# Gate and up products by seven block products instead of eight, with the activations in token halves

## The chip, the cores and the metric

One core of one Trainium2 chip runs the kernel. The metric is the device time in microseconds (us); the kernel before has a median of 1925.08 us over three runs (1923.73 to 1928.44).

## The reference, cut to what matters

A decoder trunk of two layers on 512 tokens with 1024 channels, float32. Each layer is a half-step FFN, an attention, and a half-step FFN, so there are four FFNs, which carry most of the arithmetic:

```python
x = x + 0.5 * swiglu(rms_norm(x, gain), w_gate_up, w_down)      # four times
h = rms_norm(x, gain)                                            # ahead of each attention
x = x + stick_breaking_attention(h, ...)   # layer 0
x = x + sliding_window_attention(h, ...)   # layer 1

def swiglu(h, w_gate_up, w_down):          # 1024 -> 2 x 2816 -> 1024
    gate, up = jnp.split(h @ w_gate_up, 2, axis=-1)
    return (jax.nn.silu(gate) * up) @ w_down
```

## The kernel before, in words

Activations stand transposed: 8 tiles of 128 channels x 512 tokens. Every float32 operand is split exactly into a high and a low part, and a product of two operands is three passes on TensorE (PE): high x high, high x low, low x high. The weights are the stationary operand, the tokens stream past them, 512 a matmul.

Weights come as a stream of units of 128 x 1024 (512 KB). SyncE (SP) issues the load of a unit into a `raw` tile, ScalarE (ACT) copies it to the high part `whi` (L181), VectorE (DVE) subtracts for the low part `wlo` (L186; in the attentions two halves on GpSimd (POOL), L184). There are three buffers of each; `release`, called after the last matmul of a unit, starts the work on the unit three further on. So ACT and DVE prepare one unit while PE works on another.

An FFN (`ffn`) runs over 22 columns f of 128 hidden channels. For each there is a gate and an up product, each 8 channel tiles x 3 passes = 24 matmuls of 128 x 512 into one PSUM bank (`gu`). `swiglu` then multiplies both by the row factor of the norm `rbc` (L307, L309), takes silu on ACT, multiplies (L310) and splits the result into `hh` and `hl` (L313, L314). After all columns come 8 output tiles `dn` of 22 x 3 matmuls, each added to x (L300). `norm_tile` splits each new x tile into `xh` (L252, ACT) and `xl` (L253, DVE) and adds up its squares (L260 on ACT, L261 on POOL for the first six tiles). The row factor is made late: `norm_rows` sums squares on PE (`ss`) and takes the reciprocal root in eleven small DVE operations (`nv`, `nr`, `nt`); `norm_bcast` spreads it over the partitions (`dgh`, `dgl`, `bc`, `rbc`). One 24-matmul product stands between `ss` and `bc` to cover that.

The order on PE is the program's order. On the other engines a scheduler orders the instructions by when their inputs come.

Of the kernel before, what the change touches and what calls it, by code (L numbers as in the profile page):

```python
# [22 lines left out]
DOWN = (8, 7, 7)  # L23
# [5 lines left out]
UNITS = 3  # L29
WARM = 40  # L30
# [9 lines left out]
# 500000 ** (-arange(0, 16, 2) / 16) in float32  # L40
# [24 lines left out]
class _Ordered:  # L65
    """an engine whose instructions stay in the order of the program"""
# [40 lines left out]

class _Trunk:
    def __init__(self, tc, pools, psum, aps):
        self.tc, self.nc = tc, _Engines(tc)  # L110
        self.const, self.work = pools
        self.psum = psum
        self.aps = aps
        self.units = []
        self.raw, self.ready = [], []
        self.taken = self.spent = 0
        self.roped = False
        self.extra = -1

# [28 lines left out]
    def queue(self, ap, pool=False):  # L148
        self.units.append((ap, ap.shape[1], pool))

    def _load(self, pieces=1):
        n = len(self.raw)
        if n < len(self.units):
            ap = self.units[n][0]
            raw = self.work.tile([P, ap.shape[1]], F32, tag="raw", name=f"raw{n}", bufs=UNITS)
            self.raw.append(raw)
            if pieces == 1:
                self.nc.sync.dma_start(raw, ap)

    def _open(self, n):  # L160
        size = self.units[n][1]
        hi = self.work.tile([P, size], F32R, tag="whi", name=f"whi{n}", bufs=UNITS)
        lo = self.work.tile([P, size], F32R, tag="wlo", name=f"wlo{n}", bufs=UNITS)
        self.ready.append((hi, lo))

    def advance(self, hi, lo):
        """one more unit of the weight stream ahead, in tiles that the stage has free"""
        n = self.extra = len(self.ready)
        self.ready.append((hi, lo))
        self._part(n)  # L170
        self._load()

    def _part(self, n, i=0, pieces=1):
        nc, (ap, size, pool) = self.nc, self.units[n]
        size //= pieces
        s = slice(i * size, (i + 1) * size)
        hi, lo = self.ready[n]
        raw = self.raw[n]
        if pieces > 1:
            nc.sync.dma_start(raw[:, s], ap[:, s])  # L180
        nc.scalar.copy(hi[:, s], raw[:, s])  # L181
        if pool and pieces == 1:
            for t in (slice(0, size // 2), slice(size // 2, size)):
                nc.gpsimd.tensor_sub(lo[:, t], raw[:, t], hi[:, t])  # L184
        else:
            nc.vector.tensor_sub(lo[:, s], raw[:, s], hi[:, s])  # L186

    def release(self, count):
        self.spent += count
        ahead = UNITS + (self.spent <= self.extra)  # L190
        while count and len(self.ready) < min(self.spent + ahead, len(self.units)):
            n = len(self.ready)
            self._open(n)
            self._part(n)
            self._load()

    def weights(self, a):
# [3 lines left out]
        h3, l3 = (t.rearrange("p (a b) -> p a b", a=a) for t in (hi, lo))  # L201
        return [(h3[:, i, :], l3[:, i, :]) for i in range(a)]

# [1 line left out]
    def setup(self, which):  # L205
# [4 lines left out]
        bank = self.psum.tile([P, T], F32, tag="tr", name="warmup", bufs=2)  # L210
# [5 lines left out]
        for n in range(UNITS):  # L216
            self._load(2)
            self._open(n)
        for half in range(2):
            for m in range(4):  # L220
                k = 4 * half + m
                nc.sync.dma_start(self.x[k], aps["xt"][k])
                if m < UNITS:
                    self._part(m, half, 2)
                self.norm_tile(k, which)
        for _ in range(UNITS):
            self._load()
# [16 lines left out]
    def norm_tile(self, k, which):  # L244
        nc, w = self.nc, self.work
        if k == 0:
            self.xh, self.xl = [], []
            self.acc = w.tile([P, T], F32, tag="acc", name="acc", bufs=1)
        g = self.gain[:, which * KD + k : which * KD + k + 1]
        hi = w.tile([P, T], F32R, tag=f"xh{k}", name=f"xh{k}", bufs=1)  # L250
        lo = w.tile([P, T], F32R, tag=f"xl{k}", name=f"xl{k}", bufs=1)
# [3 lines left out]
        self.xl.append(lo)  # L255
        if k == 0:
            nc.scalar.activation(self.acc, self.x[k], AF.Square)
        else:
            sq = w.tile([P, T], F32, tag="rbc", name="sq", bufs=1)
            nc.scalar.activation(sq, self.x[k], AF.Square)  # L260
            (nc.gpsimd if k < POOL_SQUARES else nc.vector).tensor_add(self.acc, self.acc, sq)  # L261

# [10 lines left out]
    def norm_rows(self):  # L273
# [4 lines left out]
        v = w.tile([P, TB], F32, tag="nv", name="nv", bufs=1)  # L278
        r = w.tile([P, TB], F32, tag="nr", name="nr", bufs=1)
        tmp = w.tile([P, TB], F32, tag="nt", name="nt", bufs=1)  # L280
# [4 lines left out]
    def norm_bcast(self):  # L285
        nc, w = self.nc, self.work
        bc = self.psum.tile([P, T], F32, tag="tr", name="bc", bufs=2)
# [8 lines left out]
        self.rbc = w.tile([P, T], F32, tag="rbc", name="rbc", bufs=1)  # L296
# [6 lines left out]
    def swiglu(self, fp, f, gu):  # L303
        nc = self.nc
        g = fp.tile([P, T], F32, tag="g", name="g", bufs=2)
        u = fp.tile([P, T], F32, tag="u", name="u", bufs=2)
        nc.vector.tensor_mul(g, gu[0], self.rbc)  # L307
        nc.scalar.activation(g, g, AF.Silu)
        nc.vector.tensor_mul(u, gu[1], self.rbc)  # L309
        nc.vector.tensor_mul(u, g, u)  # L310
        hi = fp.tile([P, T], F32R, name=f"hh{f}")
        lo = fp.tile([P, T], F32R, name=f"hl{f}")
        nc.scalar.copy(hi, u)  # L313
        nc.vector.tensor_sub(lo, u, hi)  # L314
        return hi, lo

    def ffn(self, following, first=False, rope=False):
        tc, nc = self.tc, self.nc
        with tc.tile_pool(name="ffn", bufs=1) as fp:
            hs, evac = [], []  # L320
            xs = list(zip(self.xh, self.xl))
            ahead = []
            if first:
                ahead = [(self.bank("gu"), self.weights(KD)) for _ in range(3)]
                for half in range(2):
                    ks = range(half * KD // 2, (half + 1) * KD // 2)
                    for k, (m, (ps, w)) in [(k, t) for k in ks for t in enumerate(ahead)] if half == 0 else [
                        (k, t) for t in enumerate(ahead) for k in ks
                    ]:
                        self.mm3(ps, [(w[k], xs[k])], first=(k == 0), last=(k == KD - 1), release=1 if k == KD - 1 else ())  # L330
                        if k == KD - 1 and m == 1:
                            self.norm_rows()
                ahead = [ps for ps, _ in ahead]
            for f in range(NF):
                gu = []
                for s in range(2):
                    u = 2 * f + s
                    if ahead:
# [691 lines left out]
```

## Time and profile before

| what | value |
|---|---|
| median of three runs | 1925.08 us |
| span of the profiled execution | 1925.5 us |
| PE busy / DVE / ACT / POOL, share of the span | 98% / 50% / 36% / 9% |
| mean granted TensorE clock | 0.992 |
| one FFN's gate/up products behind the first column | 228.5 us |
| one FFN's down products | 123.2 us |

The profiled execution's span and the median of the runs differ by 0.4 us, so sums against the span can be set beside the median as they are. A matmul's duration in the profile is longer than its spacing, since matmuls overlap; times per matmul are taken from the length of a run of them, not from the mean duration.

### The profile page before, as it was taken

How to read it: one execution, taken by the hardware profiler on the slowest of the kernel's cores; microseconds unless marked ns; L12 is line 12 of the kernel's file. 1: busy time of each engine (PE TensorE's matmuls, PEld its weight loads, DVE VectorE, ACT ScalarE, POOL GpSimd, SP SyncE). 2: the span in 40 equal slices, each digit the busy share in tenths (PEclk: the TensorE clock that was granted, in tenths of full speed). 3: DMA queues.
4: the chain of work that ended last, by engine and by line, in shares of the span. 5: the costliest groups of instructions: out<-in, count | busy, mean ns of one | idle time of the engine just before them, and what ended most of it. 6: DMA issues, size and time to landing. Idle time of an engine off the chain costs nothing.

```text
span 1925.5 us, 22581 instructions
## 1 busy us (share of the span) xinstructions
PE 1895.7 (98%) x8994; PEld 1565.6 (81%) x8994; DVE 970.5 (50%) x1535; ACT 695.1 (36%) x1071; POOL 172.0 (9%) x131
## 2 busy tenths in 40 slices
PE   9999999999999999999999999999998999999999
PEld 7888888877887888888888888888887788888887
DVE  6444433378887644443235444423588664444321
ACT  5333222266675323332223333222357542223211
POOL 1000000233321000000000000000142210000000
PEclk9999999999999999999999999999989999999999
DMA  5233333321112333223333222333221122332331
GB/s 167 98 97 99 96 91 92 103 69 56 49 62 66 99 97 97 92 97 94 97 96 99 92 98 96 93 93 100 81 67 34 29 92 98 99 99 90 103 109 60
DMA packets 49930, 170.52 MB, mean 89 GB/s; under 512 B 5921, under 2 KB 6177, under 8 KB 49825
## 3 DMA queue, kind: packets, MB, share of 16 engines
q1 hardware_dynamic: 49824, 169.07, 27.9%
q8 instruction: 71, 1.16, 0.2%
q14 instruction: 35, 0.28, 0.0%
HBM read 166.96 MB, written 2.10 MB: 88 GB/s over the span
## 4 chain that ended last, share of the span: by engine, by line
PE 84%; DVE 8%; issue 4%; ACT 3%; POOL 1%; DMA 0%; SPq 0%; ACTq 0%; DVEq 0%; POOLq 0%
PE gu L75 49%; PE dn L75 23%; PE op L75 4%; PE tok L75 3%; DVE keep L459 2%; DVE beta L460 1%; PE pv L75 1%; DVE qs L376 1%; DVE wt L482 1%; ACT keep L453 1%; PE sc L75 1%; PE z L75 0%; PE ptr L75 0%; DVE e L793 0%; PE q L75 0%
## 5 line engine op out<-in xcount | busy, mean ns | idle before, releaser
L181 ACT CAST whi<-raw 128x1024 fp32r<-128x1024 f32 (+2 forms) x323 | 330.0, 1022 | 964.8 <-issue 361.6
L75 PE MATMUL gu<-xh,whi 128*128 128x512 f32 x1400 | 545.5, 390 | 1.4 <-ACT whi L181 1.4
L75 PE MATMUL gu<-xh,wlo 128*128 128x512 f32 x1400 | 545.0, 389 | 0.7 <-DVE wlo L186 0.7
L75 PE MATMUL gu<-xl,whi 128*128 128x512 f32 x1400 | 544.8, 389 | 0.5 <-DVE xl L253 0.5
L186 DVE TENSOR_TENSOR wlo<-raw,whi 128x1024 fp32r<-128x1024 f32 (+2 forms) x293 | 349.4, 1193 | 248.2 <-ACT whi L181 245.6
L75 PEld LDWEIGHTS gu<-xh,wlo 128*128 128x128 f32 x1400 | 262.8, 188 | 56.5 <-DVE wlo L186 1.8
L75 PEld LDWEIGHTS gu<-xh,whi 128*128 128x128 f32 x1400 | 262.9, 188 | 56.2 <-ACT whi L181 1.9
L75 PEld LDWEIGHTS gu<-xl,whi 128*128 128x128 f32 x1400 | 262.9, 188 | 55.3 <-DVE xl L253 0.9
L75 PE MATMUL dn<-hh,wlo 128*128 128x512 f32 x704 | 280.9, 399 | 0.0
L75 PE MATMUL dn<-hl,whi 128*128 128x512 f32 x704 | 277.4, 394 | 0.0
L75 PE MATMUL dn<-hh,whi 128*128 128x512 f32 x704 | 276.0, 392 | 0.0
L309 DVE TENSOR_TENSOR u<-gu,rbc 128x512 f32<-128x512 f32 x87 | 60.1, 691 | 274.7 <-PE gu L75 274.7
L75 PEld LDWEIGHTS dn<-hl,whi 128*128 128x128 f32 x704 | 132.1, 188 | 34.3
L75 PEld LDWEIGHTS dn<-hh,whi 128*128 128x128 f32 x704 | 132.2, 188 | 31.5
L75 PEld LDWEIGHTS dn<-hh,wlo 128*128 128x128 f32 x704 | 132.2, 188 | 30.5
L307 DVE TENSOR_TENSOR g<-gu,rbc 128x512 f32<-128x512 f32 x88 | 60.8, 691 | 176.5 <-PE gu L75 176.4
L261 POOL TENSOR_TENSOR acc<-acc,sq 128x512 f32<-128x512 f32 x30 | 46.4, 1547 | 1116.1 <-ACT sq L260 1116.1
L184 POOL TENSOR_TENSOR wlo<-raw,whi 128x512 fp32r<-128x512 f32 x60 | 87.5, 1483 | 164.9 <-ACT whi L181 164.9
L75 PE MATMUL tok<-whi,xh 128*128 128x256 f32 x288 | 86.4, 300 | 0.0
L75 PE MATMUL tok<-whi,xl 128*128 128x256 f32 x288 | 82.4, 286 | 0.1
L75 PE MATMUL tok<-wlo,xh 128*128 128x256 f32 x288 | 82.3, 286 | 0.1
L300 DVE SCALAR_TENSOR_TENSOR x<-dn,x 128x512 f32<-128x512 f32 x32 | 22.1, 691 | 116.5 <-PE dn L75 116.5
(310 smaller groups left out, 1957.4 us busy)
## 6 DMA issues: line engine op xcount, KB each, us to landing
raw<-in_gu_dram SPq DMA_DIRECT2D x173, 512.0 KB, 3.4
raw<-in_dn_dram SPq DMA_DIRECT2D x64, 448.0 KB, 3.3
raw<-in_dn_dram SPq DMA_DIRECT2D x32, 512.0 KB, 3.5
raw<-in_sbqk_dram SPq DMA_DIRECT2D x16, 512.0 KB, 3.4
raw<-in_swin_dram SPq DMA_DIRECT2D x10, 512.0 KB, 3.5
raw<-in_sbv_dram SPq DMA_DIRECT2D x8, 512.0 KB, 3.3
raw<-in_sbo_dram SPq DMA_DIRECT2D x8, 512.0 KB, 3.5
raw<-in_swo_dram SPq DMA_DIRECT2D x8, 512.0 KB, 3.3
```

What stands on the lines that cost most here:

```text
L75: return self._tc.keep_in_program_order(method(*args, **kwargs))
L181: nc.scalar.copy(hi[:, s], raw[:, s])
L184: nc.gpsimd.tensor_sub(lo[:, t], raw[:, t], hi[:, t])
L186: nc.vector.tensor_sub(lo[:, s], raw[:, s], hi[:, s])
L261: (nc.gpsimd if k < POOL_SQUARES else nc.vector).tensor_add(self.acc, self.acc, sq)
L300: self.nc.vector.scalar_tensor_tensor(self.x[n], ps, factor, self.x[n], ALU.mult, ALU.add)
L307: nc.vector.tensor_mul(g, gu[0], self.rbc)
L309: nc.vector.tensor_mul(u, gu[1], self.rbc)
L376: nc.vector.tensor_sub(out[other, h, :], src[own, :], out[own, h, :])
L453: nc.scalar.activation(keep[:, :, :n], z[:, :, :n], AF.Sigmoid, scale=-0.125)
L459: nc.vector.tensor_tensor_scan(rev, rev, rev, 1.0, ALU.mult, ALU.bypass)
L460: nc.vector.tensor_mul(beta[:, :, : n - 1], beta[:, :, : n - 1], keep[:, :, 1:n])
```

## The change

The gate/up product of a column is written as a 2 x 2 block product: the rows of the weights are gate and up, the inner blocks are the even and the odd channel tiles, the columns are the first and the last 256 tokens. One level of Strassen's scheme (Winograd's form, with running sums in PSUM) needs seven block products instead of eight. Each is 4 channel tiles x 3 passes = 12 matmuls, now of 128 x 256, so a column has 84 matmuls of 256 tokens for 48 of 512. Four weight sums per column (`s0` to `s3`) are made on POOL, and all seven weight blocks are split, in slots of 128 x 512 that hold high and low part side by side (eight slots ahead in an FFN, six outside).

```diff
+    def queue_quads(self, gate, up):
...
+        return {
+            1: (quad(g, 0), (g,), False, g),
+            2: (quad(g, 1), (g,), False, g),
+            4: (quad(u, 1), (u,), False, None),
+            5: (summed(0), (), False, g),
+            6: (summed(1), (), False, g),
+            3: (summed(3), (), False, g),
+            7: (summed(2), (), False, g),
+        }
+    def make_sums(self, g):
...
+        nc.gpsimd.tensor_add(s[0], a21, a22)
+        nc.gpsimd.tensor_sub(s[1], s[0], a11)
+        nc.gpsimd.tensor_sub(s[3], a12, s[1])
+        nc.gpsimd.tensor_sub(s[2], a11, a21)
+    def _split(self, hi, lo):
...
+        self.nc.scalar.copy(hi, src)
+        (self.nc.gpsimd if pool else self.nc.vector).tensor_sub(lo, src, hi)
```

The results of a column leave PSUM in half tiles (three copies on ACT, products 1, 5 and 6, then DVE):

```diff
+    def after(self, p, f):
...
+        if p in (1, 6, 5):
+            nc.scalar.copy(r, ps["c" if p == 5 else "a"])
...
+        elif p == 2:
+            nc.vector.tensor_add(g[:, :W2], ps["b"], self.cells["r1", f])
+        elif p == 3:
+            nc.vector.tensor_add(g[:, W2:], ps["c"], self.cells["r6", f])
+            nc.vector.tensor_mul(g, g, self.rbc)
+            nc.scalar.activation(g, g, AF.Silu)
+        elif p == 7:
+            nc.vector.tensor_add(h[:, W2:], ps["a"], self.cells["r5", f])
+            nc.vector.tensor_mul(h[:, W2:], h[:, W2:], self.cells["g", f][:, W2:])
+        else:
+            nc.vector.tensor_mul(h[:, :W2], ps["a"], self.cells["g", f][:, :W2])
...
+            nc.scalar.copy(both[:, 0, :], h)
+            nc.vector.tensor_sub(both[:, 1, :], h, both[:, 0, :])
```

Ahead of an FFN `norm_quad` makes, for each pair of x tiles, the token-half sums and splits of all of them (on DVE 2 products with the gain, 7 operations of 128 x 256 and 2 of 128 x 512 a pair; before, two `xl`). The first two columns start together (`intro`: products 1, 5, 2 of both, channel tile by channel tile), then `ss`, product 6 of both, `bc`. The down product comes in two halves of 11 columns each, one after column 11 and one at the end, and the row factor of the up part is applied there (`t = dn * 0.5 * rbc`, then x + t). Product 4 of a column is put behind product 5 of the next. All tiles that PE reads now lie at one remainder of 512 bytes in their partition (192); before, the weights and xh, xl lay at 96 and hh, hl at 192.

Three places where the order moves. In the steady part of the second FFN one column (two units of the stream) took these rows of DVE before:

```order
L186 TENSOR_TENSOR wlo_5990<-raw_5880,whi_5989 128x1024
L309 TENSOR_TENSOR u<-gu,rbc 128x512
L310 TENSOR_TENSOR u<-g,u 128x512
L186 TENSOR_TENSOR wlo_6021<-raw_5921,whi_6020 128x1024
L314 TENSOR_TENSOR hl_6033<-u,hh_6032 128x512
L307 TENSOR_TENSOR g<-gu,rbc 128x512
```

One column of DVE after, at the same place, with `slot` for a weight block (split from a `raw` tile or from a sum: `s_112_7656` to `s_112_7658` are s1, s2 and s3 of one column) and a, b, c for the PSUM tiles; two more splits stand ahead of these rows:

```order
L263 TENSOR_TENSOR slot_7715<-raw_7442,slot_7715 128x512
L573 TENSOR_TENSOR h<-a,g 128x256
L263 TENSOR_TENSOR slot_7734<-s_112_7656,slot_7734 128x512
L577 TENSOR_TENSOR hs_7738<-h,hs_7738 128x512
L263 TENSOR_TENSOR slot_7753<-raw_7480,slot_7753 128x512
L561 TENSOR_TENSOR g<-b,r_7700 128x256
L263 TENSOR_TENSOR slot_7773<-s_112_7658,slot_7773 128x512
L564 TENSOR_TENSOR g<-c,r_7758 128x256
L565 TENSOR_TENSOR g<-g,rbc 128x512
L263 TENSOR_TENSOR slot_7790<-s_112_7657,slot_7790 128x512
L569 TENSOR_TENSOR h<-a,r_7720 128x256
L570 TENSOR_TENSOR h<-h,g 128x256
```

Six operations, two of them of 1024 elements, have become fourteen: seven splits and two more operations of 512, five of 256, and those that read PSUM stand behind splits in one queue.

On POOL nothing stood in an FFN before but the `acc` additions of the squares at its end; after, every column has these four rows (here s0, s2, s1, s3):

```order
L208 TENSOR_TENSOR s_110_7517<-raw_7442 128x512
L211 TENSOR_TENSOR s_110_7519<-rawx_7342,raw_7442 128x512
L209 TENSOR_TENSOR s_110_7518<-s_110_7517,rawx_7342 128x512
L210 TENSOR_TENSOR s_110_7520<-rawx_7342,s_110_7518 128x512
L208 TENSOR_TENSOR s_112_7655<-raw_7580 128x512
```

The fifth row is the next column's s0: the sums follow each other without a pause in the queue.

At the start of the third FFN, where PE has the `ss` matmuls and then a cover until `bc`, DVE had before, from the last additions of squares on:

```order
L300 SCALAR_TENSOR_TENSOR x_118<-dn,x_118 128x512
L186 TENSOR_TENSOR wlo_7486<-raw_7396,whi_7485 128x1024
L253 SCALAR_TENSOR_TENSOR xl_7493<-x_118,gain,xh_7492 128x512
L261 TENSOR_TENSOR acc<-acc,sq 128x512
L281 TENSOR_SCALAR nv<-ss 128x4
L266 TENSOR_SCALAR nr<-nv 128x4
L267 TENSOR_SCALAR nr<-nr 128x4
L269 SCALAR_TENSOR_TENSOR nt<-nr 128x4
```

and after, from the end of the last x tile's split on:

```order
L370 TENSOR_TENSOR xt_10727<-xt,xt_10726 128x512
L263 TENSOR_TENSOR slot_10882<-s_164_10606,slot_10882 128x512
L263 TENSOR_TENSOR slot_10885<-s_164_10605,slot_10885 128x512
L263 TENSOR_TENSOR slot_10888<-s_166_10681,slot_10888 128x512
L263 TENSOR_TENSOR slot_10891<-s_166_10680,slot_10891 128x512
L263 TENSOR_TENSOR slot_10894<-raw_10499,slot_10894 128x512
L561 TENSOR_TENSOR g<-b,r_10899 128x256
L561 TENSOR_TENSOR g<-b,r_10905 128x256
L414 TENSOR_SCALAR nv<-ss 128x4
L263 TENSOR_TENSOR slotx_10967<-raw_10676,slotx_10967 128x512
L401 TENSOR_SCALAR nr<-nv 128x4
L402 TENSOR_SCALAR nr<-nr 128x4
```

Five splits, whose slots come free only while PE works on the first two columns, and two half-tile additions now stand ahead of `nv`; the matmuls that cover the reciprocal root on PE were 24 of 512 tokens and are 24 of 256.

More of the change, by code (lines that the diff above doesn't have):

```diff
@@ L145, in bank, with queue @@
         return self.psum.tile([P, T], F32, tag="mm", name=name, bufs=3)
[L148 to L163, printed above, removed]
+    def queue(self, ap, pool=False, column=None):
+        n = len(self.loads)
+        self.loads.append((ap, column is not None))
+        self.uses.append(2)
+        for h in range(2):
+            self.plan.append((lambda n=n, h=h: self.raws[n][:, h * SLOT : (h + 1) * SLOT], (n,), pool, column))
@@ new lines, in _ring, with pump @@
+    def _ring(self, rings, free, own):
+        best = None
+        for r in rings if own else rings[:1]:
+            e = r.evicts()
+            if e is None:
+                return r
+            if free(e) and (best is None or e < best.evicts()):
+                best = r
+        return best
+    def pump(self, loads=1 << 30, slots=1 << 30):
+        moved = True
+        while moved:
+            moved = False
+            n = len(self.raws)
+            if loads and n < len(self.loads):
+                ap, own = self.loads[n]
+                r = self._ring(self.raw_rings, lambda e: self.uses[e] == 0, own)
+                if r:
+                    raw = r.take(n, [P, 2 * SLOT], F32)
+                    self.raws.append(raw)
+                    self.nc.sync.dma_start(raw, ap)
+                    loads -= 1
+                    moved = True
+            n = len(self.ready)
+            if slots and n < len(self.plan) and self._loaded(*self.plan[n]):
+                r = self._ring(self.slot_rings, lambda e: e < self.spent, self.plan[n][3] is not None)
+                if r:
+                    slot = r.take(n, [P, 2, SLOT], F32R)
+                    self._split(slot[:, 0, :], slot[:, 1, :])
+                    slots -= 1
+                    moved = True
@@ new lines, in _loaded @@
+    def _loaded(self, source, reads, pool, column):
+        if column is not None and column >= 0 and column not in self.sums:
+            if self.fp and column + 1 < len(self.raws):
+                self.make_sums(column)
+            elif not reads:
+                return False
+        return max(reads, default=-1) < len(self.raws)
+    def _split(self, hi, lo):
+        source, reads, pool, _ = self.plan[len(self.ready)]
+        src = source()
+        self.nc.scalar.copy(hi, src)
+        (self.nc.gpsimd if pool else self.nc.vector).tensor_sub(lo, src, hi)
+        for n in reads:
+            self.uses[n] -= 1
@@ L188, in release @@
-    def release(self, count):
[L189 to L197, printed above, removed]
+        for h in range(2):
+            s = slice(h * SLOT, (h + 1) * SLOT)
+            self._split(hi[:, s], lo[:, s])
+        self.pump()
+    def release(self, count):
+        self.spent += 2 * count
+        self.pump()
@@ new lines, in ffn_plan, with column, products, intro @@
+    def ffn_plan(self, stage):
+        gate, up, down = (self.aps[k][stage] for k in ("gate", "up", "dn"))
+        steps = []
+        def column(f):
+            return self.queue_quads(gate[f], up[f])
+        def products(*which):
+            for p, f in which:
+                self.plan.append(self.columns[stage, f][p])
+                steps.append(("product", p, f))
+        def intro(f):
+            products((1, f), (5, f), (2, f), (1, f + 1), (5, f + 1), (2, f + 1))
+            steps[-6:] = [("intro", f)]
+            products((6, f), (6, f + 1))
+            steps.append(("bcast",))
+            products((3, f), (7, f), (3, f + 1), (7, f + 1), (4, f), (4, f + 1))
+        for f in range(2):
+            self.columns[stage, f] = column(f)
+        intro(0)
+        last = None
+        for f in range(2, NF):
+            self.columns[stage, f] = column(f)
+            if last is None:
+                products((1, f), (5, f), (2, f), (6, f), (3, f), (7, f))
+            else:
+                products((1, f), (5, f), (4, last), (6, f), (2, f), (3, f), (7, f))
+            last = f
+            if f in (HALF, NF - 1):
+                half = f // HALF - (f == NF - 1)
+                half = 0 if f == HALF else 1
+                for u in range(KD * HALF // 8):
+                    at = len(self.plan)
+                    self.queue(down[half, u], column=-1)
+                    if u == 0:
+                        self.plan.insert(at + 1, self.columns[stage, f][4])
+                steps.append(("down", half, f))
+                last = None
+        return steps
@@ new lines, in open_ffn, with close_ffn, product @@
+    def open_ffn(self, pool):
+        self.fp = pool
+        self.raw_rings.append(_Ring(pool, "rawx", 1))
+        self.slot_rings.append(_Ring(pool, "slotx", MORE_SLOTS))
+    def close_ffn(self):
+        self.fp = None
+        self.raw_rings.pop()
+        self.slot_rings.pop()
+    def product(self, out, w, p, ks, first=True):
+        for k in ks:
+            (wh, wl), (xh, xl) = w[k], self.ops[p][k]
+            for i, (l, r) in enumerate(((wh, xh), (wh, xl), (wl, xh))):
+                self.nc.tensor.matmul(
+                    out, l, r, start=(first and k == i == 0), stop=(k == KD // 2 - 1 and i == 2), skip_group_check=not first,
+                )
@@ new lines, in taken_slot, with ffn @@
+    def taken_slot(self):
+        self.spent += 1
+        self.pump()
+    def ffn(self, stage, steps, following, rope=False):
+        nc, fp = self.nc, self.fp
+        with self.tc.tile_pool(name="psf", bufs=1, space=bass.MemoryType.PSUM) as ps:
+            self.psum = ps
+            if stage == 0:
+                self.setup(0)
+            self.cells = {}
+            self.hs = {}
+            for step in steps:
+                if step[0] == "product":
+                    _, p, f = step
+                    self.run_product(p, f)
+                    if rope and (p, f) == (7, NF // 2 + 3):
+                        self.rope_tables()
+                elif step[0] == "intro":
+                    f0 = step[1]
+                    ws = {}
+                    for f in (f0, f0 + 1):
+                        for p in (1, 5, 2):
+                            ws[f, p] = self.slot()
+                    for f, k in ((f0, 0), (f0, 1), (f0 + 1, 0), (f0 + 1, 1), (f0, 2), (f0 + 1, 2), (f0, 3), (f0 + 1, 3)):
+                        for p in (1, 5, 2):
+                            self.product(self.cell(p, f), ws[f, p], p, (k,))
+                    for _ in range(6):
+                        self.taken_slot()
+                    for f in (f0, f0 + 1):
+                        for p in (1, 5, 2):
+                            self.after(p, f)
+                    self.norm_rows()
+                elif step[0] == "bcast":
+                    self.norm_bcast(fp, 1)
+                else:
+                    self.down(step[1], step[2], following)
@@ new lines, in down @@
+    def down(self, half, late, following):
+        nc = self.nc
+        at, w = 0, []
+        for n in range(KD):
+            ps = self.psum.tile([P, T], F32, tag="bc"[n % 2], name="dn", bufs=2)
+            for i in range(HALF):
+                if at % 4 == 0:
+                    w = self.slot()
+                (wh, wl), (hh, hl) = w[at % 4], self.hs[half * HALF + i]
+                self.mm(ps, wh, hh, start=(i == 0), stop=False)
+                self.mm(ps, wh, hl, start=False, stop=False)
+                self.mm(ps, wl, hh, start=False, stop=(i == HALF - 1))
+                at += 1
+                if at % 4 == 0:
+                    self.taken_slot()
+                if at == 4:
+                    self.run_product(4, late)
+            t = self.fp.tile([P, T], F32, tag="h", name="t", bufs=2)
+            nc.vector.scalar_tensor_tensor(t, ps, 0.5, self.rbc, ALU.mult, ALU.mult)
+            nc.vector.tensor_add(self.x[n], self.x[n], t)
+            if half:
@@ L816, in window_values @@
         if b == 0:
-            os[c] = [ap.tile([P, 2, T], F32R, name=f"o{s}{c}") for s in "hl"]
+            os[c] = [self.work.tile([P, 2, T], F32R, tag=f"ob{2 * c + i}", name=f"o{i}{c}", bufs=1) for i in range(2)]
         oh, ol = os[c]
@@ new lines, in build, with feed @@
+        for n in range(KD):
+            net.queue(aps["swo"][n])
+        steps[3] = net.ffn_plan(3)
+        def feed(fp, first, stages, last):
+            net.open_ffn(fp)
+            if first:
+                with_out, psum = first
+                with_out(lambda n: net.norm_quad(n, 3 * (stages[0] // 2) + 2 * (stages[0] % 2)))
+                psum.close()
+            for i in stages:
+                nxt = last if i == stages[-1] else lambda n, j=i + 1: net.norm_quad(n, 3 * (j // 2) + 2 * (j % 2))
+                net.ffn(i, steps[i], nxt, rope=i == 2)
+            net.close_ffn()
```

334 lines of the change are left out of this document (171 added, 163 removed).

## The prediction

> **What bounds the kernel now.** I read the page first: engine shares, then the chain that ended last.
>
> ```profile
> PE 1895.7 (98%) x8994; PEld 1565.6 (81%) x8994; DVE 970.5 (50%) x1535; ACT 695.1 (36%) x1071; POOL 172.0 (9%) x131
> PE gu L75 49%; PE dn L75 23%; PE op L75 4%; PE tok L75 3%; DVE keep L459 2%; DVE beta L460 1%; PE pv L75 1%; DVE qs L376 1%; DVE wt L482 1%; ACT keep L453 1%; PE sc L75 1%; PE z L75 0%; PE ptr L75 0%; DVE e L793 0%; PE q L75 0%
> ```
>
> TensorE is busy in 98% of the span, and the gate/up products (`gu`) are half of the chain. The chain in order of time gives the price of a matmul of each shape, since these stretches run without a gap:
>
> ```profile
> 386.68 11.53 PE tok L75 x96
> 879.91 123.21 PE dn L75 x528
> 1015.45 228.48 PE gu L75 x1008
> ```
>
> 228.48 / 1008 = 0.2267 us for a gate/up matmul of 512 tokens; 123.21 / 528 = 0.2333 us for a down matmul; 11.53 / 96 = 0.1201 us for one of 256. A matmul of 256 costs 53% of one of 512, not 50%. The table by stage shows what the other engines do meanwhile (columns: stretch, length, then busy time and count of PE, PEld, DVE, ACT, POOL):
>
> ```profile
> 0.00:32.88 32.88, 29.31 (x147) 23.61 (x148) 23.64 (x42) 19.55 (x33) 9.19 (x14) 1.00 0.63 209
> 606.84:639.02 32.18, 32.18 (x139) 25.95 (x139) 21.44 (x24) 16.24 (x24) 7.58 (x5) 1.00 0.32 98
> 651.40:879.91 228.51, 228.51 (x1010) 189.20 (x1009) 108.09 (x137) 70.15 (x89) 0.00 (x0) 1.00 0.30 96
> 1003.12:1015.45 12.33, 12.33 (x60) 10.28 (x59) 7.43 (x21) 4.98 (x9) 0.00 (x0) 1.00 0.27 85
> ```
>
> In the gate/up stage (third row) DVE is half idle and POOL does nothing. That idle time is what the change spends.
>
> **Term 1, the matmuls.** Before: 4 FFNs x 22 columns x 48 = 4224 x 0.2267 = 957.6 us. After: 4 x 22 x 84 = 7392 x 0.1201 = 887.8 us. Gain 69.8 us. Each matmul loads its own weights, but so do the 0.1201 us ones, so loads are no new limit. Neighbouring rows of 256 lie within 0.003 us of that, 22 us either way. The Trainium skill, "TensorE: Matmul & The Clock Gate", section "Wait — 56ns, not 53.3ns?", gives a warm spacing of N / 2.4 GHz plus about 2.5 ns, so 109.2 and 215.8 ns; by it the term would be an estimated 104 us. The rows here show 13 ns over N / 2.4 GHz for both shapes, and the sum goes by them.
>
> **Term 2, one remainder.** Gate/up operands (weights and `xh`) already lie at one remainder, the down operands do not, and a down matmul takes 6.6 ns more. If that is the reason, 4 x 528 = 2112 of them gain 14 us; the new remainder is another one than the 96 of `gu`, and no row has it for this shape, so the other end is 0. I take 7.
>
> **Term 3, the columns.** This decides. A column has 84 x 0.1201 = 10.09 us of PE. The durations come from these rows (DVE with 512 elements, then 256, ACT with 512, then the spacing of queued operations):
>
> ```profile
> L314 DVE TENSOR_TENSOR hl<-u,hh x88: 680/686/693, 35.1 to 1801.7; 128x512 fp32r<-128x512 f32 x88
> ...
> L756 DVE TENSOR_TENSOR q<-tok,qgain x16: 393/419/426, 1389.0 to 1469.8; 128x256 f32<-128x256 f32 x16
> ...
> L313 ACT CAST hh<-u 128x512 fp32r<-128x512 f32 x88 | 54.7, 621 | 62.1 <-DVE u L310 62.1
> ...
> 31.61 0.69 DVE L307 TENSOR_TENSOR g<-gu,rbc 128x512 f32<-128x512 f32 x1
> 32.22 0.68 DVE L309 TENSOR_TENSOR u<-gu,rbc 128x512 f32<-128x512 f32 x1
> 32.81 0.68 DVE L307 TENSOR_TENSOR g<-gu,rbc 128x512 f32<-128x512 f32 x1
> ```
>
> Starts are 0.60 us apart, 0.08 less than the duration, so 256 elements cost 0.34. Nine operations of 512 and five of 256 make 9 x 0.60 + 5 x 0.34 = 7.1 us. That alone would fit. But POOL now adds 4 sums a column, and the trace shows that POOL and DVE exclude each other where both read two operands from SBUF:
>
> ```profile
> 12.81 0.68 DVE L186 TENSOR_TENSOR wlo<-raw,whi 128x512 fp32r<-128x512 f32 x1
> ...
> 13.08 1.56 POOL L261 TENSOR_TENSOR acc<-acc,sq 128x512 f32<-128x512 f32 x1 [0.74 <-ACT sq L260]
> ...
> 13.65 1.54 DVE L253 SCALAR_TENSOR_TENSOR xl<-x,gain,xh 128x512 fp32r<-128x512 f32 x1 [0.16 <-ACT xh L252]
> 15.12 0.68 DVE L186 TENSOR_TENSOR wlo<-raw,whi 128x512 fp32r<-128x512 f32 x1
> ...
> L253 DVE SCALAR_TENSOR_TENSOR xl<-x,gain,xh x48: 737/746/1797, 4.8 to 1559.7; 128x512 fp32r<-128x512 f32 x48
> ...
> L376 DVE TENSOR_TENSOR qs<-qf,qs x16: 684/687/1686, 388.8 to 555.2; 64x512 fp32r<-64x512 f32 x16
> ...
> L184 POOL TENSOR_TENSOR wlo<-raw,whi x60: 1264/1298/2280, 364.9 to 1431.7; 128x512 fp32r<-128x512 f32 x60
> ...
> L300 DVE SCALAR_TENSOR_TENSOR x<-op,x x16: 674/688/694, 612.5 to 1557.7; 128x512 f32<-128x512 f32 x16
> ```
>
> `xl` takes 0.74 us alone and 1.54 beside an `acc`; `qs` 0.69 alone and up to 1.69. The time beside POOL is the own time plus what is left of POOL's operation, up to 1.0 us. `x<-op`, with one operand in PSUM, never stretches. So a sum costs DVE at most 1.3 us (POOL's whole duration) and at least nothing, where it falls into a wait of DVE; I take 1.0, the `qs` row, since DVE will seldom wait here. Of the fourteen operations four read PSUM and can run under a sum; four sums that alternate with splits meet about one of them. 7.1 + 4 x 1.0 - 0.3 = 10.8 us a column, against 10.09 on PE and 228.5 / 21 = 10.88 before. ACT has seven casts, a silu and a split of 512 and three half copies, by 0.62 us (`hh`) under 7 us: it fits.
>
> The slots are eight ahead, but that does not save it: evacuations stand in DVE's one queue behind splits, and product 4 waits for product 7's evacuation two products (2.9 us) earlier. So PE can run only 2.9 us ahead of DVE. Eleven columns stand in each half, with the sums of two made during the down products ahead: 9 x 0.7 = 6.3 us lost in each of 8 halves, less 2.9 us in the four that follow a down half with DVE at rest: 50 - 12 = 38 us. Bounds: 0 (10.09) and 8 x 9 x 2.2 = 158 (sums at 1.3, nothing under them).
>
> **Term 4, the start.** The chain and DVE there, before:
>
> ```profile
> 30.39 0.45 PE bc L75 x2
> 30.84 2.04 PE gus L75 x9
> ...
> 24.14 0.16 DVE L281 TENSOR_SCALAR nv<-ss 128x4 f32<-128x4 f32 x1 [0.64 <-PE ss L75]
> ...
> 29.03 1.13 DVE L293 SCALAR_TENSOR_TENSOR dgl<-ident,nr,dgh 128x128 fp32r<-128x128 f32 x4
> ```
>
> At 30.84 us PE has done 87 matmuls, 19.7 us of work: 11 us lost. After, DVE has ahead of `nv` 14 slot splits and 10 more operations of 512, 8 products with the gain (one source; between `nv`'s 0.16 us and 0.69, say 0.4) and 30 of 256: 24 x 0.60 + 3.2 + 30 x 0.34 = 28 us, and POOL 13 additions of up to 1.0. From 4 us on, with landings and ACT between, `nv` comes at about 41 and `bc` 6.2 later (24.14 to 30.39), at 47, when PE has done 96 matmuls of 256, 11.5 us: 35 lost. Cost 24 us; bounds 12 (no addition of POOL in the way) and 30.
>
> **Term 5, FFNs behind an attention (two).** DVE's queue from the first residual (612.5 us in the L300 row, L300's first `op`) to `nv` now holds 74 operations, 35 us by the same prices, and POOL 14 additions. Before, DVE was busy 21.4 of 32.2 us there. `ss` would be due at 639.0 + 8.6 = 647.7, 35 us later. 35 + 14 less some 4 under the residuals is 45, so `nv` is 10 us late; then 5.5 us of root and `dgl` meet a cover of 2.9. I take 11 us each, 22; bounds 3 and 16 each.
>
> **Term 6, the third FFN.** DVE keeps pace with the down products. But the five splits ahead of `nv` wait for slots that PE frees only 7 to 8.6 us into the FFN, then 3.0 us, 0.7 for the two additions and some of POOL's 4: `nv` 5 us behind `ss`, and 5.5 against a cover of 2.9. Before, PE was busy in all of this stretch (the fourth row of the table). Cost 7; bounds 3 and 10.
>
> **Nothing or little.** DMA: 1 MB per 10 us, no more bytes than before, at 96 GB/s against 209 at the start. The second evacuation operation of `dn` hides under 7.6 us of matmuls, and adds 0.6 us after the last. Splits of 512 in the attentions for 1024: 1 us in all.
>
> **Sum.** -69.8 - 7 + 38 + 24 + 22 + 7 + 1 = +15, so 1940 us, against a profiled span of 1925.5 (median 1925.1).
>
> **Rivals.** (B) PE sets the pace in the columns after all. It does once a sum costs DVE less than (10.09 - 7.1) / 4 = 0.75 us; when DVE has to wait for PE, sums fall into those waits, which favours it, and the queue through which evacuations and splits alternate speaks against it. Then term 3 is 0: 1902 us, and with a full term 2 and small start terms 1880. Faster. (C) Nothing hides and POOL's holds are longer, 1.0 to 1.3 us each: 11.1 to 12.3 a column, term 3 at 64 to 150 us, 1966 to 2050. The `wlo` row at 1.30 speaks for it, `qs` against. By the Trainium skill, "SBUF — State Buffer", section "SBUF: two separate sides", the two engines share a port pair that is locked for a whole instruction, so the loser waits it out; that agrees with the stretch of `xl` and `qs`, and puts the price at C's end. (D) Half matmuls run nearer to half the time than `tok` does (0.112 at the shortest): with the other terms as forecast 1885 to 1915 if PE were the bound, nothing otherwise.
>
> **How the numbers follow.** Forecast 45% (own range 1919 to 1962), B 36%, C 14%, D 5%. About 0.3% (6 us) is what a measurement can tell from no change. Faster: B, D and a little of the forecast, 0.41; within: 0.11, of the forecast's low end; slower: 0.48. The range from B's middle to C's middle: 1880 to 1990.
>
> **What would show it.** Term 1: a run of product matmuls without a gap at 0.120 each. Term 2: `dn` at 0.2267 or 0.2333. Term 3: splits beside sums at 1.5 to 1.7 us, PE in the columns waiting for DVE (`h`, `g`) or for ACT's copies behind it, columns at 10.8. Terms 4 to 6: PE idle ahead of `bc`, with DVE without a pause. I am wrong if DVE shows pauses of a microsecond in the columns while PE shows none, or if POOL's sums lie beside stretched splits only rarely.

## The result, and the profile after

The kernel after takes 2033.5 us (median of four runs, 2031.25 to 2033.86) beside 1925.2 us for the kernel before: a ratio of 1.0556, 95% interval 1.0541 to 1.0571. The profiled execution spans 2029.5 us, 104.0 more than before. The forecast was 1940 and its range ended at 1990: the side was right, the size was not.

The page of the kernel after, engine shares and the chain that ended last:

```profile
PE 1847.6 (91%) x12162; PEld 1677.1 (83%) x12162; DVE 1620.8 (80%) x2576; ACT 966.4 (48%) x1950; POOL 703.5 (35%) x483
PE 50%; DVE 37%; ACT 6%; issue 5%; DMA 1%; POOL 1%; DVEq 0%; ACTq 0%; SPq 0%; POOLq 0%
```

PE has gone from 98% to 91% of a longer span, DVE from 50% to 80%, and 37% of the chain is DVE's. Three columns in the third FFN (the table by stretch, columns as in the prediction; the last three numbers are PE's granted clock, DMA's share and GB/s), then POOL's operations there and a piece of the timeline (start, duration, engine, line, operation):

```profile
1140.00:1174.00 34.00, 31.06 (x254) 30.45 (x253) 33.32 (x43) 17.39 (x36) 18.41 (x14) 1.00 0.29 97
```

```profile
1138.97 1.28 POOL L208 TENSOR_TENSOR s<-rawx 128x512 f32<-128x512 f32 x1 [5.27 <-DMA rawx<-in_up_dram]
...
1150.27 1.28 POOL L208 TENSOR_TENSOR s<-raw 128x512 f32<-128x512 f32 x1 [5.18 <-DMA raw<-in_up_dram]
...
1161.57 1.29 POOL L208 TENSOR_TENSOR s<-rawx 128x512 f32<-128x512 f32 x1 [5.19 <-DMA rawx<-in_up_dram]
```

```profile
1152.03 1.78 DVE L263 TENSOR_TENSOR slotx<-s,slotx 128x512 fp32r<-128x512 f32 x1
...
1153.23 1.72 POOL L209 TENSOR_TENSOR s<-s,raw 128x512 f32<-128x512 f32 x1
...
1153.73 0.41 DVE L569 TENSOR_TENSOR h<-a,r 128x256 f32<-128x256 f32 x1
...
1154.25 0.98 DVE L570 TENSOR_TENSOR h<-h,g 128x256 f32<-128x256 f32 x1
...
1155.03 1.36 POOL L210 TENSOR_TENSOR s<-raw,s 128x512 f32<-128x512 f32 x1
1155.16 1.78 DVE L263 TENSOR_TENSOR slotx<-raw,slotx 128x512 fp32r<-128x512 f32 x1
1156.86 0.68 DVE L263 TENSOR_TENSOR slot<-s,slot 128x512 fp32r<-128x512 f32 x1
```

DVE is busy in 33.3 of 34 us, PE is not. The first sums of successive columns start 11.3 us apart: that is the column (forecast 10.8, PE alone 10.09, before 10.88). Each sum holds one DVE operation: a split of 0.68 takes 1.78, a product of 256 elements 0.98 for 0.41. The operation with one operand in PSUM (`h<-a,r`) keeps its 0.41. POOL itself rests 5.2 us a column, until the next `raw` tile has landed.

The starts of the FFNs grew too. The chain around the first root, the spread of the row factor behind the first attention (timeline), and PE's clock at the start (by stretch):

```profile
46.12 1.84 PE ss L79 x8
47.95 5.17 PE a L79 x24
...
53.50 0.63 ACT slotx L262
54.15 1.15 DVE slotx L263
55.29 1.15 DVE nr L402
...
56.51 1.14 DVE nt L404
...
61.92 1.28 PE bc L79 x2
```

```profile
716.08 1.27 POOL L208 TENSOR_TENSOR s<-raw 128x512 f32<-128x512 f32 x1 [6.10 <-DMA raw<-in_up_dram]
716.13 5.25 DVE L426 SCALAR_TENSOR_TENSOR dgl<-ident,nr,dgh 128x128 fp32r<-128x128 f32 x4 [0.53 <-ACT dgh L425]
...
717.30 1.32 POOL L211 TENSOR_TENSOR s<-raw,raw 128x512 f32<-128x512 f32 x1
718.58 1.31 POOL L209 TENSOR_TENSOR s<-s,raw 128x512 f32<-128x512 f32 x1
719.96 1.26 POOL L210 TENSOR_TENSOR s<-raw,s 128x512 f32<-128x512 f32 x1
```

```profile
0.00:30.00 30.00, 10.10 (x60) 8.55 (x60) 26.44 (x35) 14.53 (x28) 19.51 (x21) 0.64 0.44 158
30.00:66.00 36.00, 19.19 (x101) 18.22 (x102) 31.90 (x86) 12.53 (x29) 14.97 (x10) 0.64 0.13 45
```

`bc` comes at 61.9 us (forecast 47, before 30.4). Operations of the root on four elements, `nr` and `nt`, take 1.15 us where they meet a POOL addition. The four `dgl` of 128 x 128 took 1.13 us in the kernel before and take 5.25 here: four operations, four sums, one for one. And TensorE's granted clock is 0.64 in the first 66 us, in which PE is busy for only 29.

For the accounts below each FFN is cut at two points, read from the timeline: from the end of the work before it to the first silu ("lead"), and from there to the last down matmul.

| us | FFN 0 | attention 0 | FFN 1 | FFN 2 | attention 1 | FFN 3 |
|---|---|---|---|---|---|---|
| before | 373.3 | 265.3 | 364.1 | 364.0 | 190.5 | 364.0 |
| after | 412.3 | 272.2 | 387.0 | 375.5 | 191.9 | 385.8 |
| of which lead | 67.3 | | 42.3 | 30.4 | | 40.8 |

### The profile page after: what moved, and what is told of

It is laid out like the page before. It is cut to its first block, busy times and chain, and to the rows that moved or that the text cites. A ratio compares the mean times of both kernels' runs of the same rounds, so it can differ in the third digit from the quotient of the medians.

```text
span 2029.5 us, 31712 instructions
## 1 busy us (share of the span) xinstructions
PE 1847.6 (91%) x12162; PEld 1677.1 (83%) x12162; DVE 1620.8 (80%) x2576; ACT 966.4 (48%) x1950; POOL 703.5 (35%) x483
## 4 chain that ended last, share of the span: by engine, by line
PE 50%; DVE 37%; ACT 6%; issue 5%; DMA 1%; POOL 1%; DVEq 0%; ACTq 0%; SPq 0%; POOLq 0%
PE dn L79 22%; DVE slot L263 11%; PE a L79 9%; PE c L79 5%; DVE slotx L263 5%; DVE g L565 4%; PE tok L79 4%; PE b L79 3%; PE op L79 2%; DVE hs L577 2%; DVE keep L696 2%; ACT hs L576 1%; PE pv L79 1%; DVE g L564 1%; DVE h L569 1%
## 5 line engine op out<-in xcount | busy, mean ns | idle before, releaser
L79 PE MATMUL a<-xt,slot 128*128 128x256 f32 x2580 | 343.3, 286 | 56.8 <-DVE h L569 36.9
L79 PEld LDWEIGHTS a<-xt,slot 128*128 128x128 f32 x2580 | 320.4, 191 | 71.4 <-DVE h L569 47.3
L79 PE MATMUL dn<-hs,slot 128*128 128x512 f32 x1560 | 360.5, 389 | 0.0
L79 PEld LDWEIGHTS dn<-hs,slot 128*128 128x128 f32 x1560 | 291.9, 188 | 60.0
L263 DVE TENSOR_TENSOR slot<-raw,slot 128x512 fp32r<-128x512 f32 x289 | 252.5, 876 | 89.8 <-ACT slot L262 89.3
L262 ACT CAST slot<-raw 128x512 fp32r<-128x512 f32 x349 | 214.6, 618 | 193.3 <-PE dn L79 143.1
L263 DVE TENSOR_TENSOR slot<-s,slot 128x512 fp32r<-128x512 f32 x253 | 241.9, 958 | 32.5 <-ACT slot L262 32.4
L262 ACT CAST slot<-s 128x512 fp32r<-128x512 f32 x253 | 152.6, 619 | 125.9 <-PE a L79 51.3
L79 PE MATMUL dn<-hs,slotx 128*128 128x512 f32 x552 | 130.1, 389 | 0.0
L79 PE MATMUL tok<-slot,xs 128*128 128x256 f32 x864 | 116.8, 289 | 0.9 <-DVE t L601 0.9
```

The source lines that it names most:

```text
L79: return self._tc.keep_in_program_order(method(*args, **kwargs))
L262: self.nc.scalar.copy(hi, src)
L263: (self.nc.gpsimd if pool else self.nc.vector).tensor_sub(lo, src, hi)
```

## The experiments

Theory 1 is that POOL's sums and DVE exclude each other. Its price of 1.05 us of DVE per sum is (11.3 - 7.1) / 4, so it puts all of the column beyond DVE's own 7.1 us down to the sums. The rivals are that a column's chain of dependent steps sets the pace, and that DVE's own operations do.

**The sums on DVE.** All four `nc.gpsimd` of `make_sums` become `nc.vector`.

```diff
-        nc.gpsimd.tensor_add(s[0], a21, a22)
+        nc.vector.tensor_add(s[0], a21, a22)
```

> Exclusion (theory 1: each POOL sum holds DVE off for about 1.05 us, whatever DVE would have done): a sum on DVE costs it 0.60, so DVE has 7.1 + 4 x 0.60 = 9.5 us a column, under PE's 10.09. Columns of 10.1 instead of 11.3, some 8 x 10 x 1.2 = 95 us less, and 0.4 us less for each of the 13 or 14 additions ahead of the root at the start and behind the attentions, 5 us each: 1920 to 1940. Round trip (theory 2: PE waits for the chain PSUM copy - add - product - split of a column, not for DVE's total): columns stay at 11.3 or grow, 2030 to 2060. Count (theory 3: DVE's own operations and their order make the 11.3, POOL is innocent): 2.4 us more a column, 13.7, about 2200.

1986.1 us, ratio to the kernel before 1.0309 (1.0292 to 1.0326). That DVE does four operations more and the kernel is 47 us faster rules out the count. But the time is not in theory 1's 1920 to 1940 either. Columns are 10.6, not 10.1: DVE is busy in 29.7 of 31.8 us (three columns, the row), and the rest goes in short waits for ACT's copies and PE, so it was not to be packed without gaps.

```profile
1109.80:1141.60 31.80, 31.04 (x254) 30.43 (x254) 29.74 (x56) 18.63 (x36) 0.00 (x0) 1.00 0.31 99
```

**The sums made once.**

```diff
+        if self.kept:
+            self.sums[g] = self.kept
...
+            return
```

> The four weight sums are made for the first column of each FFN pool only and used for all its columns (the computed values are other ones; all other work is there). Exclusion: DVE has 7.1 us a column, PE sets the pace at 10.1: about 95 us less in the columns and some 5 to 15 us less at the second and third FFN and behind the attentions, 1910 to 1935. Round trip: 2030, as with the sums. Count: 2030.

1926.5 us, ratio 1.0001 (0.9991 to 1.0010). Columns of 10.1 in all eight halves, PE without a pause (40.00 of 40.00 us):

```profile
1250.00:1290.00 40.00, 40.00 (x336) 40.00 (x335) 31.55 (x57) 24.89 (x48) 0.00 (x0) 1.00 0.29 94
```

**POOL fills the sum tiles instead of adding.**

```diff
-        nc.gpsimd.tensor_add(s[0], a21, a22)
...
+        for t in s:
+            nc.gpsimd.memset(t, 0.02)
```

> POOL fills the four sum tiles of each column with a constant, so it writes as much and at the same places but reads nothing (the computed values are other ones). If what excludes is POOL's reading from SBUF: splits at 0.68 us again, columns at 10.1, 1910 to 1935 as without sums. If a POOL operation holds DVE off whatever it does, by its duration: half to all of the loss stays, 1980 to 2035.

1914.3 us, ratio 0.9936 (0.9921 to 0.9950). POOL still makes 352 writes of 128 x 512, but a split of a sum is back at 0.69 us (0.96 in the kernel after). By line and shape, the kernel after first:

```profile
L263 DVE TENSOR_TENSOR slot<-s,slot 128x512 fp32r<-128x512 f32 x253 | 241.9, 958 | 32.5 <-ACT slot L262 32.4
```

```profile
L209 POOL MEMSET s<- 128x512 f32 x352 | 183.9, 525 | 939.3 <-DVE slot L261 718.7 <-DVE slotx L261 205.2 <-ACT slot L260 11.2
L261 DVE TENSOR_TENSOR slot<-s,slot 128x512 fp32r<-128x512 f32 x253 | 173.8, 689 | 86.0 <-ACT slot L260 86.0
```

So it is POOL's reading from SBUF that excludes. The Trainium skill, "SBUF — State Buffer", section "SBUF: two separate sides", has this condition for a DVE operation with two SBUF inputs; these rows agree. The kernel is 12 us faster than with the sums made once: 4.4 of it in the first lead, where real sums were still made, about 7 in the attentions, which I did not trace further.

**The kernel before with one remainder.** The three tiles `nv`, `nr`, `nt` are taken ahead of the stream's tiles, so `hh` and `hl` lie at 192 like the weights.

```diff
+        self.small = [c.tile([P, TB], F32, name=nm) for nm in ("nv", "nr", "nt")]
...
-        v = w.tile([P, TB], F32, tag="nv", name="nv", bufs=1)
...
+        v, r, tmp = self.small
```

> The kernel before with the three small tiles of the root moved ahead of the stream's tiles, so that all operands of PE lie at remainder 192 of 512 bytes, hh and hl too. If the two remainders make a down matmul 0.2333 instead of 0.2267: 2112 x 0.0066 = 14 us less, 1911. If the layout has no part in it (the down products' own accumulation or weights would have): 1925.

1913.1 us, ratio 0.9933 (0.9918 to 0.9948): 13.3 us less. The 528 down matmuls went from 123.21 us to (chain)

```profile
250.80 119.68 PE dn L75 x528
```

0.2267 each. Term 2 alone is worth taking. This small change of the kernel before is the fastest version here that still computes the trunk, and beats both kernels.

**Each sum twice.**

```diff
+        for _ in range(2):
+            nc.gpsimd.tensor_add(s[0], a21, a22)
...
```

> Each of POOL's four sums of a column is made twice in a row (the second writes the same values again). If each holds DVE off for 1.05 us and nothing hides: DVE has 7.1 + 8 x 1.05 = 15.5 us a column instead of 11.3, 4.2 us more in 80 columns = 336, and about 40 more at the starts of the FFNs (the 41 us by which the sums lengthened them, once more): 2370 to 2440. If the column were set by another wait and POOL's work were hidden up to its own length (8 x 1.5 = 12 us): 2090 to 2130. If POOL and DVE strictly alternated so that DVE pays each POOL operation in full, 1.5 us: 7.1 + 12 = 19 us a column, 2650.

2429.2 us, one run. In the second half of an FFN, where no start is mixed in, the nine columns take 140.7 us: 15.6 each, against 98.5 / 9 = 10.9 with single sums and 90.6 / 9 = 10.1 with none. The time fits theory 1's range, but that is luck: DVE is not what sets the pace here. Two columns (by stretch), then one column of the chain:

```profile
1341.00:1373.30 32.30, 19.60 (x132) 19.17 (x132) 23.24 (x28) 11.30 (x23) 23.34 (x17) 0.82 0.20 65
```

```profile
1344.42 3.93 DMA raw<-in_up_dram
...
1348.49 1.83 POOL s L209
...
1357.10 0.63 ACT slot L263
...
1358.88 1.76 DVE slot L264
...
1360.67 3.29 DMA rawx<-in_up_dram
```

DVE is busy in 23.2 of 32.3 us only. From 1348.5 to 1357.1 the chain is POOL's sums one behind the other; then come a copy, a split, and the load of the next `raw` tile, for which POOL waits. So the 4.7 us that four more sums cost are no measure of what a sum costs DVE.

**Half of each sum.**

```diff
+        v = slice(0, W2)
+        for t in s:
+            nc.gpsimd.memset(t[:, W2:], 0.02)
+        nc.gpsimd.tensor_add(s[0][:, v], a21[:, v], a22[:, v])
...
```

> POOL adds only the first 256 of the 512 elements of each sum and fills the others with a constant (the computed values are other ones); filling alone cost nothing. If a sum holds DVE off in proportion to its elements: some 0.5 us each, DVE 7.1 + 2.1 = 9.2 us a column, under PE's 10.1; columns of 10.1 to 10.5 and half of the 41 us at the starts: 1930 to 1960. If the cost belongs to the instruction, not to its length (1.05 us each): 2010 to 2035.

1937.6 us, one run, columns of 10.1 and PE busy throughout. The price goes with the elements read, not with the instruction: a split beside a half sum takes 1.22 us, 0.53 more than alone, where one beside a whole sum takes 1.78, 1.1 more (by stretch, then the timeline):

```profile
1120.00:1140.00 20.00, 20.00 (x169) 20.00 (x169) 18.67 (x28) 12.46 (x25) 10.54 (x16) 1.00 0.39 118
```

```profile
1125.18 1.22 DVE L266 TENSOR_TENSOR slot<-raw,slot 128x512 fp32r<-128x512 f32 x1
```

**Four additions per column in the kernel before.**

```diff
+        for j in range(4):
+            nc.gpsimd.tensor_add(extra, u, self.x[j])
```

> The kernel before with four POOL additions of 128 x 512 per column added, whose result nobody uses (u + x tile, after hl). DVE has 5.2 us a column there (108.1 of 228.5 us) and would have 5.2 + 4 x 1.05 = 9.4 of 10.88: the stretched splits are seen in the trace, the time stays: 1925 to 1931. If a hold reaches PE other than through DVE's total (a late split, a late hl): 1 to 2 us a column, 1990 to 2100.

1927.6 us, ratio 1.0002 (0.9992 to 1.0012). The same additions, and no time: `hl` goes from 686 ns (the prediction's row) to 1743, but DVE's busy time grows only from 970.5 to 1102.4 us (the page, then a row by line and shape):

```profile
PE 1895.2 (98%) x8994; PEld 1565.0 (81%) x8994; DVE 1102.4 (57%) x1535; ACT 695.0 (36%) x1071; POOL 798.4 (41%) x483
```

```profile
L314 DVE TENSOR_TENSOR hl<-u,hh 128x512 fp32r<-128x512 f32 x88 | 153.4, 1743 | 4.1 <-ACT hh L313 4.1
```

That is 132 / 352 = 0.37 us a sum; the rest fell into DVE's waits.

**Gain on ACT**, beside the sums on DVE.

```diff
-        nc.vector.tensor_scalar(xg, self.x[n], g, None, ALU.mult)
+        nc.scalar.activation(xg, self.x[n], AF.Copy, scale=g)
```

> Sums on DVE, and the eight products with the gain ahead of an FFN on ACT instead of DVE. If DVE's queue ahead of the root sets the starts of the FFNs (PE waits 7 to 8 us for the first operands behind an attention and 3 to 4 us for bc): 8 x 0.40 = 3.2 us less at the start and at two others, 1 at the third FFN, 1974 to 1982 against 1986 with sums on DVE alone. If ACT's copies set them: 1986 or up to 5 us more.

1980.0 us, ratio 1.0269 (1.0253 to 1.0285), 6 us less than with the sums on DVE alone, as expected if DVE's queue ahead of the root counts. In the profiled executions, though, the leads give only 0.8, 1.7, -1.1 and 1.4 us of it, where 3.2 at three of them and 1 at the third FFN were expected; where the rest lies I did not trace.

**No token-half differences**, beside POOL filling.

```diff
-            nc.vector.tensor_sub(t[:, 0, :], xg[:, W2:], xg[:, :W2])
...
-            part((th[:, 2:, :], tl[:, 2:, :]), t)
```

> On the kernel in which POOL only fills the sum tiles (1914): the four differences of token halves per pair of x tiles are left out as well, products 4 to 7 read the halves of product 1 (the computed values are other ones; PE's work and order stay). Six DVE operations of 256 and one of 512 less per pair, 4 x (6 x 0.34 + 0.60) = 10.6 us less ahead of each root. If DVE's own work ahead of the root makes the rest of the loss at the FFNs' starts: first silu 7 to 10 us earlier at the start and behind both attentions, 1 to 4 at the third FFN, 1882 to 1894. If the chain x tile - ACT copy - DVE - PE of one tile, or the root's eleven small operations, make it: 1908 to 1915.

1889.2 us, ratio 0.9805 (0.9786 to 0.9825), 25 us less. The leads, by FFN:

| lead, us | FFN 0 | FFN 1 | FFN 2 | FFN 3 |
|---|---|---|---|---|
| after | 67.3 | 42.3 | 30.4 | 40.8 |
| POOL fills only | 50.6 | 32.9 | 22.7 | 33.2 |
| and no token-half differences | 41.0 | 24.0 | 23.3 | 27.4 |

So the new work there carries 24 us even without a POOL addition in its way. It is not DVE's alone: a pair of x tiles has seven operations less on DVE and three copies less on ACT. The third FFN gave nothing; the 1 to 4 us expected there were wrong.

**PE kept busy in its pauses**, beside sums on DVE and gain on ACT. The first line stands ahead of an FFN's first product, the second ahead of `bc`; the numbers are matmuls by FFN.

```diff
+                    self.fill((0, 120, 20, 120)[stage])
...
+                    self.fill((110, 90, 60, 90)[stage])
```

> On the kernel with sums on DVE and gain on ACT (1980): PE's pauses ahead of an FFN's first product (8 us behind the attentions, 2 at the third FFN) and ahead of bc (4 to 7 us) are filled with matmuls of 128 x 128 zeros that nobody uses. In the trace the granted clock behind such pauses is 0.5 to 0.6 for about 4 us. If PE sets the pace there, each of seven pauses of 4 us and more costs some 1.7 us (4 x 0.43) that the filling gives back: 9 to 12 us less, 1967 to 1972. If DVE sets the pace behind the pause, PE only waits longer at the next one: 1977 to 1983.

1982.4 us, ratio 1.0295 (1.0279 to 1.0311): no gain. PE's timeline shows why: the first filling itself stood behind a wait and came when the pause was over.

```profile
661.79 1.07 PE L79 MATMUL op<-o,slot 128*128 128x512 f32 x4
670.81 5.39 PE L79 MATMUL fill<-warm 128*128 128x128 bf16 x71 [7.95 <-DVE x L433]
```

The second alone:

> As before, but only the pauses ahead of bc are filled: in the run with both, the filling ahead of an FFN's first product stood behind the wait for the attention's last output (DVE x) and came after the pause, 6 us too late. If PE sets the pace behind bc: full clock there instead of 0.5, some 2 us in each of three FFNs and up to 5 in the first (whose end came 4.8 us earlier with both), 8 to 11 us less than 1980: 1969 to 1972. If DVE sets the pace: 1978 to 1982.

1968.7 us, ratio 1.0222 (1.0206 to 1.0239), 11.3 us less than 1980.0. Behind `bc` of the second FFN, unfilled and filled (by stretch, the clock third from the end):

```profile
700.50:704.50 4.00, 4.00 (x17) 3.81 (x18) 1.20 (x3) 0.22 (x1) 0.00 (x0) 0.50 0.00 0
```

```profile
693.50:697.50 4.00, 4.00 (x30) 3.75 (x31) 2.63 (x6) 1.60 (x2) 0.00 (x0) 1.00 0.00 0
```

17 matmuls in 4 us became 30. In the profiled spans (1977.0 and 1967.0) the four FFNs gained 4.9, 0.2, 0.1 and 3.0 us and the first attention 1.8. The total fits the theory that PE sets the pace. But the leads, where the filling acts, are only 1.3, 1.7, 2.0 and 1.3 us shorter, some 6 in all; in the second and third FFN they were lost again in the columns, as the other theory had it, and in the first and last the columns were faster by 3.6 and 1.7 us, for which I have no cause.

## Why the prediction was wrong, by its terms

The measured terms come from the two tables, with PE's pace for an FFN taken out: before 22 x 48 x 0.2267 + 528 x 0.2333 = 362.6, after 22 x 84 x 0.1201 + 528 x 0.2267 = 341.6 us. The columns' part of an FFN is what lies behind the lead, after against POOL filling (345.0 to 326.9 in the first); the start's part is the rest of the loss over PE's pace, less the loss before.

| term | forecast | measured |
|---|---|---|
| 1 matmuls | -69.8 | -69.8 (columns of 10.1 once DVE is out of the way) |
| 2 one remainder | -7 | -14 (0.2267, here and in the kernel before with one remainder) |
| 3 columns | +38 | +71 (18.1, 17.5, 17.6, 18.1) |
| 4 start | +24 | +42 (70.7 - 18.1 - 10.7) |
| 5 FFNs behind an attention | +22 | +51 (26.4 and 24.7) |
| 6 third FFN | +7 | +15 |
| little | +1 | +8 (attentions 6.9 and 1.4) |
| sum | +15 | +103 (the spans differ by 104.0) |

The down run in the chain after is 57.15 us for 252, 0.2268 each:

```profile
185.92 57.15 PE dn L79 x252
```

Terms 1 and 2 hold, the second at its far end. The mechanism of term 3 is right (splits at 1.5 to 1.7 beside sums were forecast, 1.78 came, and DVE is busy in 98% of the stretch). So is the price of the sums, taken from the timeline by when operations start: beyond the 0.60 and 0.34 us of the prediction, the held operations of a steady column lose 1.0, 1.1, 0.55 and 1.1 us, 3.7 in all, and the forecast was 4 x 1.0 - 0.3. The third sum is the cheap one since it begins under `h<-a,r`, which reads PSUM.

**The step that failed first is the 7.1 us for DVE's own operations,** which were taken to follow each other without a gap. 0.5 us a column go in short waits, most of them ahead of operations that need the result of the operation before or a copy of ACT's:

```profile
1158.40 0.68 DVE L263 TENSOR_TENSOR slot<-s,slot 128x512 fp32r<-128x512 f32 x1
1159.16 0.69 DVE L577 TENSOR_TENSOR hs<-h,hs 128x512 fp32r<-128x512 f32 x1
...
1161.31 0.42 DVE L564 TENSOR_TENSOR g<-c,r 128x256 f32<-128x256 f32 x1
1161.76 1.66 DVE L565 TENSOR_TENSOR g<-g,rbc 128x512 f32<-128x512 f32 x1
```

`hs` starts 0.76 us behind the split, not 0.60, and `g<-g,rbc` 0.45 behind `g<-c,r`, not 0.34. With the sums on DVE it is the same: 10.6 instead of 7.1 + 4 x 0.60 = 9.5. So a column is 7.1 + 3.7 + 0.5 = 11.3 for 10.8, its excess over PE 1.2 instead of 0.7: 8 x 9 x 1.2 = 86 instead of 50, of which 15 came off, where 12 had been allowed (the last column of a half takes only 9.0 to 9.1 us from silu to silu). Rival C (11.1 to 12.3 a column, 1966 to 2050, given 14%) covers both the column and the time, but by luck: part of a sum did hide, no hold in these columns was above 1.1 us, and with the starts as forecast a term 3 of 71 would have made 1973.

**The second failed step is the starts, terms 4 to 6: 108 for 53.** With POOL filling, the leads are 16.7 + 9.4 + 7.7 + 7.6 = 41 us shorter; that part is shown. Where it lies, by the timeline (the kernel after less POOL filling, `bc` by its second matmul):

| us | FFN 0 | FFN 1 | FFN 2 | FFN 3 |
|---|---|---|---|---|
| to `ss` | 10.5 | 4.7 | 5.0 | 2.1 |
| `ss` to `nv` | 0.5 | 2.2 | 2.2 | 2.2 |
| `nv` to `bc` | 5.2 | 2.4 | -0.2 | 2.8 |

More than half stands ahead of `ss`. In term 6 the sentence that failed is that DVE keeps pace with the down products. `nv` came 4.9 us behind `ss` (forecast 5) and `bc` 5.8 behind `nv` (5.5), but `ss` came 15 us after the down products instead of 8.6: PE's first product waits 4.37 us for an operation of theirs on DVE (0.88 with POOL filling) and then runs in a stretch with a clock of 0.68.

```profile
1076.27 0.59 PE L79 MATMUL a<-one,slot 128*128 128x256 f32 x3 [4.37 <-DVE t L601]
```

In terms 4 and 5 `nv` itself was late, at 50.0 for 41 us at the start and 8 to 9 us later than forecast behind the attentions, and then the root was long, which had been carried over from before. From `nv` to `bc` it took 11.9 us instead of 6.2 at the start, and 9.1 and 8.7 instead of 5.5 behind the attentions. Each of these roots met four sums, and small operations are held as long as large ones. At the start DVE also stood still for 3.2 us in this time, waiting for ACT's copies into slots.

Of the other 67 us, the run without token-half differences shows 24 to be new work on DVE and ACT. PE's low clock behind its pauses was in no term; the run that filled the pauses ahead of `bc` gained 11, some 6 of it in the leads, on another base, so these parts do not add up to a full account. What makes the rest I have not separated.

Altogether the reading of POOL's sums costs 2033.5 - 1914.3 = 119 us, and without it the seven products only reach the kernel before with one remainder (1914.3 and 1913.1). The 70 us gained on PE go into the starts.

## What to carry to other kernels

Idle time on two engines can be spent only once where both read SBUF: price a POOL operation as DVE time, and where DVE then fills the column, add the short waits of its own queue (0.5 us in 11.3 here), which a sum of operations does not have. Read the price in the stage where it will be paid: the same four additions cost nothing under a PE-bound column and 71 us where DVE has no slack. A change that gains by stage must also pay at each start: there the holds delay the operations that PE's first product waits for, and a chain of small dependent operations takes each hold in full. And a time inside the forecast of a theory is no proof of it: with each sum made twice the chain had moved to POOL and the loads.

## What the runs showed of the hardware that was not expected

An operation of 4 or 128 elements on DVE is held about as long as one of 512 (`nr` takes 1.15 us, four `dgl` 5.25, and a split 1.78 for 0.68), and a POOL operation that only writes holds nothing (`memset`, 525 ns each). An operation that reads one tile from SBUF is held too, unlike what the prediction took as the condition: the product with the gain takes 1.51 us beside a sum and 0.48 alone.

```profile
682.54 1.51 DVE L364 TENSOR_SCALAR xg<-x,gain 128x512 f32<-128x512 f32 x1
```

PE's clock is at half behind a pause, here for 3.5 us of work. In the kernel with POOL filling, behind a pause of 7 us (by stretch, then the chain, three matmuls a row):

```profile
646.00:653.00 7.00, 0.12 (x1) 0.00 (x0) 7.00 (x15) 3.33 (x7) 1.05 (x2) 0.76 0.24 75
653.00:656.50 3.50, 3.33 (x15) 3.37 (x16) 3.35 (x9) 2.06 (x4) 0.00 (x1) 0.50 0.00 0
656.50:662.00 5.50, 5.50 (x47) 5.50 (x47) 0.52 (x1) 0.27 (x1) 0.00 (x0) 1.00 0.02 3
```

```profile
654.78 0.64 PE b L79 x3
...
657.02 0.36 PE a L79 x3
```

0.64 for three turns into 0.36: this pause costs PE another 1.7 us. The Trainium skill, "TensorE: Matmul & The Clock Gate", section "What's actually happening", states half rate after an idle window of about 3.4 us and as long a busy window to leave it; these rows agree, and the prediction had not used it.

Down matmuls whose two operands lie at different remainders of 512 bytes (96 and 192) take 0.2333 us, at the same one 0.2267. Which unit of the chip makes the difference was not tried.
